# Weight sums of a seven-product matrix scheme: from VectorE additions to accumulating DMAs, with the signs of one operand row turned

## The chip, the cores and the metric

The kernel runs as one program on one core of a Trainium2 chip. The metric is the device time of one execution, in microseconds (us); lower is better. The kernel before takes 1967.14 us (median of three runs, 1966.62 to 1968.99). PE is the matrix engine, PEld its weight loads, DVE the vector engine, ACT the scalar engine, POOL the GpSimd engine and SP the engine that does nothing here but issue DMAs.

## The reference, cut to what matters

One step of a two-layer decoder trunk for 1024 prompt tokens and 8 times 8 sample tokens with the same weights, model width 1024, all in 32-bit floats. Each layer is a mixer followed by a dense SwiGLU FFN of inner width 2816. The change touches only the FFN:

```
def _swiglu_ffn(x, g, w_gate, w_up, w_down):
    h = _rmsnorm(x, g)
    return x + (jax.nn.silu(h @ w_gate) * (h @ w_up)) @ w_down
```

## The kernel before, in words

The activations lie transposed: model features on the 128 partitions, 1088 tokens (1024 + 64) along the free side. They are treated as two halves of 544 tokens, each of two chunks of 272. A first stage (up to about 390 us) does the input projection, convolution, attention and half of the output projection. After it come four passes (`half_pass`): layer 0 half 0, layer 0 half 1, layer 1 half 0, layer 1 half 1. Each pass goes through the 22 blocks of 128 FFN columns in 11 pairs j, so there are 44 pairs in all.

Every weight block is 128 x 1024 floats (512 KB). It is loaded from DRAM into a `raw` tile, and split into a high part `whi` (ACT, rounded to the float32r format) and a low part `wlo = raw - whi` (DVE). Every product is then three matmuls: high by high, high by low, low by high.

The gate and up products of one pair are computed as a Strassen-Winograd scheme. It has two halves of the contraction, two FFN blocks and two token chunks, and so 7 products where 8 would be plain. Its weight operands are A11, A12, S2, S1, S3, S4, A22. Of these A11, A12 and A22 are loaded blocks and four are sums made on DVE by whole-block operations, in `gate_up` of `Weights`: S1 = A21 + A22, S3 = A11 - A21, S2 = S1 - A11, S4 = A12 - S2. The activation operands B11, B21, T2, T1, T3, B22, T4 are made once for each pass by `operands`. One product is 2 x 4 x 3 = 24 matmuls of 272 columns.

A pair on PE is: seven products (items 0 to 6, which this text calls R11, R12, S2, S1, S3, S4, R22), then the down projection of the pair before (items D0 and D1, four groups of 12 matmuls each). That is 7 x 24 + 8 x 12 = 264 matmuls. `act` turns the results into hidden activations: for the last one, from product R22, ACT applies the silu out of PSUM (`t<-pp 128x272`), DVE multiplies (`t<-pp,t 128x272`), and the result is split into `hh` and `hl`. Each group of the down projection takes one of four PSUM tiles `pp` and is added to the residual by one DVE operation (`g<-pp,g` or `res<-pp,res`). The fourth group of a pair takes the tile that this last multiplication reads.

What sets the order: PE's order is as written. The other engines' orders come from the scheduler of the framework, which starts from program order. Each engine and each DMA queue runs in order, and waits by semaphores. There are six `whi`/`wlo` slots in rotation, so that the conversion of an item can begin once PE has finished the item six before it. `get` converts up to `LEAD` = 4 items ahead in program order. There are four `raw` tiles in rotation (pool `wraw`) and one separate tile for S1. All weight loads stand in SP's queue; a load waits until the tile that it fills has been converted. All of the trace's instructions go through a helper and so carry one line, L111; they are told apart by the names of their tiles.

Of the kernel before, what the change touches and what calls it, by code (L numbers as in the profile page):

```python
# [10 lines left out]
F32 = mybir.dt.float32  # L11
F32R = mybir.dt.float32r
BF16 = mybir.dt.bfloat16
AF = mybir.ActivationFunctionType
ALU = mybir.AluOpType
# [3 lines left out]
P = 128  # L19
# [26 lines left out]
PRE = (False, False, True, True)  # L46
NT = 7
LAG = 4000.0
LEAD = 4
NP = FT // 2  # L50
PROD = ('B11', 'B21', 'T2', 'T1', 'T3', 'B22', 'T4')
# [24 lines left out]
FFN = {}  # L76
# [4 lines left out]
POOLW = len(UNITS) + len(FFN)  # L81
OUTW = POOLW + 2


def r32(ap):
    return ap.bitcast(F32)


class Paced:
# [3 lines left out]
    def __init__(self, engine, rate, fixed):  # L93
        self.engine, self.rate, self.fixed, self.t = engine, rate, fixed, 0.0
# [20 lines left out]
class Weights:  # L115


    def __init__(self, nc, w_ap, raw_pool):
        self.nc, self.w, self.raw_pool = nc, w_ap, raw_pool
        self.slots = deque()  # L120
        self.loaded, self.next, self.ahead = deque(), 0, 1
        self.ready, self.todo, self.raws = deque(), deque(), {}

    def add_pool(self, pool, n, name):
        self.slots.extendleft((pool, f"{name}{i}") for i in range(n))
# [6 lines left out]
    def slot(self):  # L132
        pool, nm = self.slots[0]
        self.slots.rotate(-1)
        hi = pool.tile([P, 1024], F32R, tag=nm + "h", name="whi")
        lo = pool.tile([P, 1024], F32R, tag=nm + "l", name="wlo")
        return hi, lo
# [32 lines left out]
    def gate_up(self, l, j):  # L170


        r = {}

        def get(n):
            if n not in r:
                r[n] = self.raw(FFN[l, j, n])
            return r[n]

        def sums():  # L180
            for n in ('A21', 'A22'):
                get(n)
            r['S1'] = self.sums.tile([P, 1024], F32, tag="S1", name="S1")
            self.V.tensor_tensor(r['S1'], r['A21'], r['A22'], ALU.add)
            self.V.tensor_tensor(r['A21'], r['A11'], r['A21'], ALU.subtract)
            self.V.tensor_tensor(r['A11'], r['S1'], r['A11'], ALU.subtract)
            self.split(r['A11'])

        def s4():
            self.V.tensor_tensor(r['A12'], r['A12'], r['A11'], ALU.subtract)  # L190
            self.split(r['A12'])
        return [lambda: self.split(get('A11')), lambda: self.split(get('A12')), sums, lambda: self.split(r['S1']),
                lambda: self.split(r['A21']), s4, lambda: self.split(r['A22'])]

    def down(self, l, j):
        return [lambda: self.split(self.raw(FFN[l, j, 'D0'])), lambda: self.split(self.raw(FFN[l, j, 'D1']))]

    def pool(self, g):
        def f():
            t = self.raw_pool.tile([P, 1024], F32, tag="raw", name="raw")  # L200
            self.nc.sync.dma_start(out=t[:, :512], in_=self.w[POOLW + g // 2][:, g % 2 * 512:g % 2 * 512 + 512])
            self.split(t, 512)
        return [f]

    def out(self, o):
        return [lambda: self.split(self.raw(OUTW + o))]

    def advance(self):
        while self.todo and len(self.ready) < LEAD:
            self.todo.popleft()()  # L210

    def get(self):
        if not self.ready:
            self.todo.popleft()()
        u = self.ready.popleft()
        self.advance()
        return u
# [31 lines left out]
def _body(ctx, tc, I, O):  # L249
    nc = tc.nc  # L250
    V, S, T, G = Paced(nc.vector, 1.04, 175), Paced(nc.scalar, 0.85, 190), Paced(nc.tensor, 0, 0), nc.gpsimd
    cp = ctx.enter_context(tc.tile_pool(name="const", bufs=1))
    xp = ctx.enter_context(tc.tile_pool(name="xp", bufs=1))
    tp = ctx.enter_context(tc.tile_pool(name="tp", bufs=1))
    wraw = ctx.enter_context(tc.tile_pool(name="wraw", bufs=4))
    wa = ctx.enter_context(tc.tile_pool(name="wa", bufs=1))
    ps_pool = tc.tile_pool(name="ps", bufs=8, space=PSUM)
    ps = ps_pool.__enter__()
# [1 line left out]
    W = Weights(nc, I['w'], wraw)  # L260
# [5 lines left out]
    def pcol(name, i=0, n=1):  # L266
        return prm[:, PRM[name] + i:PRM[name] + i + n]
# [7 lines left out]
    def both():  # L275
        return pair_of(wide())

    def pair_of(t):
        return t[:, :2 * TW].rearrange("p (c t) -> p c t", c=2)
# [12 lines left out]
    def bank():  # L292
        return ps.tile([P, 512], F32, tag="ps", name="ps")

    def bank2():
        return pp.tile([P, 2, 512], F32, tag="pp", name="pp")[:, :, :TW]
# [426 lines left out]
    for t in range(4):  # L723
        b = bank()
# [111 lines left out]
    def rt(h, o):  # L836
        return res[h][o // 4][:, o % 4]
# [13 lines left out]
    def operands(h, goff):  # L851

        x, n = {}, {}

        def value(m, i):
            n[m] = slot(xp, i, 4, F32)
            return n[m]

        def norm(m, i, k, q):
            value(m, i)  # L860
            for j in range(4):
                kt = 4 * q + j
                V.scalar_tensor_tensor(n[m][:, j], pair_of(rt(h, kt))[:, k], pcol('norm_ffn', goff + kt), RS[h][:, k],
                                       ALU.mult, ALU.mult)

        def cut(m, i):
            x[m] = slot(xp, i, 4), slot(xp, i + 1, 4)
            split(x[m], n[m])

        def diff(m, a, b, i):  # L870
            out = n[i] if i in n else value(m, i)
            V.tensor_tensor(out, n[a], n[b], ALU.subtract)
            n[m] = out

        def job(f, *a):
            return lambda: f(*a)
        first = [job(norm, 'B11', 0, 0, 0), job(cut, 'B11', 2), job(norm, 'B21', 14, 0, 1), job(cut, 'B21', 4)]
        rest = [job(norm, 'B12', 1, 1, 0), job(diff, 'T1', 'B12', 'B11', 12), job(norm, 'B22', 10, 1, 1),
                job(diff, 'T2', 'B22', 'T1', 13), job(cut, 'T2', 6), job(cut, 'T1', 8), job(diff, 'T4', 'B21', 'T2', 0),
                job(diff, 'T3', 'B22', 'B12', 'B12'), job(cut, 'B22', 12), job(cut, 'T3', 10), job(cut, 'T4', 14)]  # L880
        return x, deque(first), deque(rest)

    hold.append(True)
    ua = W.take(4)
    for o in range(KT):
        b = bank2()
# [13 lines left out]
    for k in range(2):  # L900
        for o in range(KT):
            b = bank2()
            mm3(b[:, k], [(wcol(u, o), Y(4 + j, k)) for j, u in enumerate(uc)])
            r = pair_of(rt(0, o))[:, k]
# [9 lines left out]
            if k and o == 1:  # L914
                X, build, rest = operands(0, 0)
# [6 lines left out]


    hp = ctx.enter_context(tc.tile_pool(name="h", bufs=1, side="right"))
    W.sums = hp
    hist = [hp.tile([P, 16 + PB + TW], F32, name=f"hist{i}") for i in range(2)]
    for t in hist:
        V.memset(t[:, 0:16], 0.0)
# [4 lines left out]
    def product(out, w, x, s, start, stop):  # L933

        for kt in range(4):
            wh, wl = (t[:, s * 512 + kt * P:s * 512 + kt * P + P] for t in w)
            xh, xl = (t[:, kt, :] for t in x)
            T.matmul(out=out, lhsT=wh, rhs=xh, start=start and kt == 0, stop=False, skip_group_check=True)
            T.matmul(out=out, lhsT=wh, rhs=xl, start=False, stop=False, skip_group_check=True)
            T.matmul(out=out, lhsT=wl, rhs=xh, start=False, stop=stop and kt == 3, skip_group_check=True)  # L940

    def gate_up(x):

        h = [[hp.tile([P, 2, TW], F32R, tag="h" + n, bufs=4, name="h" + n) for n in 'hl'] for _ in range(2)]

        def keep(src):
            t = both()
            S.activation(t, src, AF.Copy)
            return t

        def act(f, k, src, kept):

            if kept is None:
                g = both()
                S.activation(g[:, 0], src[:, 0], AF.Silu)
                V.tensor_tensor(g[:, 0], src[:, 1], g[:, 0], ALU.mult)
            else:
                g = kept
                V.tensor_tensor(g, src, g, ALU.add)
                S.activation(g[:, 0], g[:, 0], AF.Silu)  # L960
                V.tensor_tensor(g[:, 0], g[:, 0], g[:, 1], ALU.mult)
            split((h[k][0][:, f, :], h[k][1][:, f, :]), g[:, 0])

        def step(i, dst=None):
            w = W.get()
            start = dst is None
            if start:
                dst = bank2()
            for s in range(2):
                product(dst[:, s], w, x[PROD[i]], s, start, True)  # L970
            flush()
            return dst
        a = step(0)
        p1 = keep(a)
        b = step(1)
        act(0, 0, b, p1)
        step(2, a)
        u2 = keep(a)
        c = step(3)
        p5 = keep(c)  # L980
# [133 lines left out]
    def half_pass(l, half, x, pooled, after, following, mixed=False):  # L1114
# [4 lines left out]
        for j in range(NP):  # L1119
# [28 lines left out]
            if j:  # L1148
                down(half, last, beside=steps)
# [157 lines left out]
```

## Time and profile before

| | |
|---|---|
| median of three runs | 1967.14 us |
| profiled execution, its own time | 1965.52 us |
| its span in the trace | 1963.7 us |
| PE busy | 1887.9 us, 96% |
| PEld busy | 1835.1 us, 93% |
| DVE busy | 1670.9 us, 85% |
| ACT busy | 940.5 us, 48% |
| POOL busy | 32.6 us, 2% |
| granted TensorE clock, mean | 0.99 |
| DMA | 177.75 MB, mean 91 GB/s |

The median and the profiled execution differ by 1.6 us. The busy shares are means over the span; the rows further below show single stretches. In the rows of waits, "PE pp <- DVE res" means that PE was idle until a DVE instruction that touches `res` released it.

### The profile page before, as it was taken

To read this page: it belongs to the slowest core of one execution; us is meant where nothing else is said; L and a number is where in the kernel's file an instruction comes from. 1 tells how busy PE (TensorE), PEld (TensorE's weight loads), DVE (VectorE), ACT (ScalarE), POOL (GpSimd) and SP (SyncE) were. 2 spreads that over 40 slices of the span, in tenths; PEclk is the share of its full clock that TensorE was granted. 3 is DMA by queue.
4 is the path that set the end of the run, shared out by engine and by line. 5 is a ranking of instruction groups with operands and counts; after the bars stand their busy time and mean duration, and the time that the engine had idled before them with its cause. 6 is when DMAs were issued, how large, how long until landed. Compare 5 with 4: busy or idle time off the path is not lost.

```text
span 1963.7 us, 34755 instructions
## 1 busy us (share of the span) xinstructions
PE 1887.9 (96%) x14437; PEld 1835.1 (93%) x14437; DVE 1670.9 (85%) x2593; ACT 940.5 (48%) x1609; POOL 32.6 (2%) x47
## 2 busy tenths in 40 slices
PE   7999889799999999899999998999999999999999
PEld 6998568799999999799999998999999999999999
DVE  6999999999778785998988889989898897778784
ACT  7345784544343453564454454544444544443432
POOL 1100000000000000000000000000000000000000
PEclk9999998899999999999999999999999999999999
DMA  5310103132232341132232321323323223232321
GB/s 194 94 59 1 47 15 110 41 99 97 88 106 86 108 156 65 44 103 97 93 112 76 113 97 44 117 90 108 106 77 114 98 93 125 89 106 86 108 86 68
DMA packets 52479, 177.75 MB, mean 91 GB/s; under 512 B 6000, under 2 KB 10704, under 8 KB 51776
## 3 DMA queue, kind: packets, MB, share of 16 engines
q1 hardware_dynamic: 50960, 172.12, 26.2%
q0 software_dynamic: 1360, 3.40, 0.9%
q8 instruction: 113, 1.85, 0.4%
q14 instruction: 46, 0.38, 0.1%
HBM read 169.74 MB, written 6.74 MB: 90 GB/s over the span
## 4 chain that ended last, share of the span: by engine, by line
PE 84%; DVE 10%; ACT 3%; DMA 2%; issue 1%; SPq 0%; ACTq 0%; DVEq 0%
PE pp L111 74%; PE ps L111 10%; DVE x L111 3%; DVE wlo L111 2%; DVE res L111 1%; DVE ca L111 1%; ACT P L111 1%; DMA raw<-w 1%; ACT t L111 1%; DVE g L111 1%; DVE raw L111 1%; DVE t L111 1%; DVE ss L111 1%; ACT x L111 0%; DMA x<-x 0%
## 5 line engine op out<-in xcount | busy, mean ns | idle before, releaser
L111 PE MATMUL pp<-x,whi 128*128 128x272 f32 x5568 | 1069.1, 291 | 25.3 <-ACT t L111 5.9
L111 PEld LDWEIGHTS pp<-x,whi 128*128 128x128 f32 x5568 | 884.5, 190 | 31.1 <-ACT t L111 7.4
L111 PE MATMUL pp<-x,wlo 128*128 128x272 f32 x2784 | 810.7, 291 | 0.6 <-DVE wlo L111 0.4
L111 ACT ACTIVATE whi<-raw 128x1024 fp32r<-128x1024 f32 (+1 forms) x390 | 407.5, 1048 | 520.4 <-PE pp L111 353.3
L111 DVE TENSOR_TENSOR wlo<-raw,whi 128x1024 fp32r<-128x1024 f32 (+1 forms) x386 | 466.5, 1212 | 113.5 <-ACT whi L111 112.6
L111 PEld LDWEIGHTS pp<-x,wlo 128*128 128x128 f32 x2784 | 528.6, 190 | 1.6 <-DVE wlo L111 1.6
L111 PE MATMUL pp<-hh,whi 128*128 128x272 f32 x1408 | 408.4, 290 | 6.6 <-DVE res L111 4.3
L111 PE MATMUL pp<-hh,wlo 128*128 128x272 f32 x1408 | 407.6, 289 | 0.0
L111 PE MATMUL pp<-hl,whi 128*128 128x272 f32 x1408 | 405.7, 288 | 0.0
L111 PEld LDWEIGHTS pp<-hh,whi 128*128 128x128 f32 x1408 | 265.3, 188 | 8.6 <-DVE res L111 4.4
L111 PEld LDWEIGHTS pp<-hl,whi 128*128 128x128 f32 x1408 | 265.4, 188 | 0.0
L111 PEld LDWEIGHTS pp<-hh,wlo 128*128 128x128 f32 x1408 | 264.9, 188 | 0.0
L111 PE MATMUL ps<-x,whi 128*128 128x272 f32 x896 | 178.5, 297 | 7.0 <-ACT whi L111 7.0
L111 DVE TENSOR_TENSOR g<-pp,g 128x544 f32<-128x544 f32 x184 | 129.9, 722 | 43.0 <-PE pp L111 42.5
L111 PEld LDWEIGHTS ps<-x,whi 128*128 128x128 f32 x896 | 143.9, 190 | 13.1 <-ACT whi L111 7.0
L111 DVE TENSOR_TENSOR res<-pp,res 128x544 f32<-128x544 f32 (+1 forms) x200 | 136.3, 698 | 13.9 <-PE pp L111 13.0
L111 DVE TENSOR_TENSOR t<-pp,t 128x544 f32<-128x544 f32 (+1 forms) x176 | 114.4, 651 | 38.5 <-PE pp L111 38.1
L111 PE MATMUL ps<-x,wlo 128*128 128x272 f32 x448 | 130.4, 291 | 0.4 <-DVE wlo L111 0.4
L111 ACT ACTIVATE hh<-t 128x272 fp32r<-128x272 f32 x176 | 74.6, 426 | 108.8 <-DVE t L111 107.9
L111 ACT ACTIVATE t<-t 128x272 f32<-128x272 f32 x170 | 71.8, 427 | 98.3 <-DVE t L111 97.7
L111 DVE TENSOR_TENSOR raw<-raw 128x1024 f32<-128x1024 f32 x88 | 107.5, 1221 | 0.0
L111 ACT ACTIVATE t<-pp 128x544 f32<-128x544 f32 (+1 forms) x176 | 96.9, 551 | 12.9 <-PE pp L111 12.8
(166 smaller groups left out, 1534.0 us busy)
## 6 DMA issues: line engine op xcount, KB each, us to landing
raw<-w SPq DMA_DIRECT2D x294, 512.0 KB, 3.3
x<-x SPq DMA_DIRECT2D x16, 272.0 KB, 8.5
res<-x SPq DMA_DIRECT2D x2, 1088.0 KB, 6.3
g<-x SPq DMA_DIRECT2D x2, 1088.0 KB, 6.0
o_y<-res SPq DMA_DIRECT2D x4, 544.0 KB, 2.7
raw<-w SPq DMA_DIRECT2D x8, 256.0 KB, 3.0
o_y<-g SPq DMA_DIRECT2D x2, 544.0 KB, 3.2
o_y<-g SPq DMA_DIRECT2D x4, 272.0 KB, 2.1
```

What stands on the lines that cost most here:

```text
L111: return f(*a, **k)
```

## The change

The four sums are no longer computed on DVE. For each sum the first block is loaded into a `raw` tile through SP's queue as before, and then a second block is added to it by a DMA that accumulates (`accum_op=add`), issued by POOL. Its source is DRAM (A22 onto A21 for S1, A21 onto A11 for S3) or another `raw` tile (S1 onto A11 for S2, S2 onto A12 for S4). So A11, A12, A21 and A22 are loaded seven times in all for one pair where they were loaded four times. Only additions occur, so signs are turned in the activations: B11 is stored negated (`cut` with sign -1), T1, T2 and T3 are formed with the other sign, and one addition in `act` becomes a subtraction.

The fetch of an item (its load and its accumulating DMA) is now separate from its conversion, and `convert` issues fetches up to `AHEAD` = 2 items in front of the conversion. The pool of `raw` tiles has five instead of four; the separate S1 tile is gone.

```diff
-        def sums():
-            for n in ('A21', 'A22'):
-                get(n)
-            r['S1'] = self.sums.tile([P, 1024], F32, tag="S1", name="S1")
-            self.V.tensor_tensor(r['S1'], r['A21'], r['A22'], ALU.add)
-            self.V.tensor_tensor(r['A21'], r['A11'], r['A21'], ALU.subtract)
-            self.V.tensor_tensor(r['A11'], r['S1'], r['A11'], ALU.subtract)
-            self.split(r['A11'])
-
-        def s4():
-            self.V.tensor_tensor(r['A12'], r['A12'], r['A11'], ALU.subtract)
-            self.split(r['A12'])
-        return [lambda: self.split(get('A11')), lambda: self.split(get('A12')), sums, lambda: self.split(r['S1']),
-                lambda: self.split(r['A21']), s4, lambda: self.split(r['A22'])]
+        def made(n, first, *added):
+            def fetch():
+                r[n] = self.raw(FFN[l, j, first])
+                for a in added:
+                    self.nc.gpsimd.dma_start(out=r[n], in_=r[a] if a in r else block(a), accum_op=ALU.add)
+            return fetch, lambda: self.split(r[n])
+        a11, a12, a22 = made('R11', 'A11'), made('R12', 'A12'), made('R22', 'A22')
+        s1, s3 = made('S1', 'A21', 'A22'), made('S3', 'A11', 'A21')
+        s2, s4 = made('S2', 'A11', 'S1'), made('S4', 'A12', 'S2')
+
+        def s1s2():
+            s1[0]()
+            s2[0]()
+        return [a11, a12, (s1s2, s2[1]), (lambda: None, s1[1]), s3, s4, a22]
...
+    def convert(self):
+
+        while self.todo and self.fetched <= AHEAD:
+            if self.fetched == len(self.todo):
+                break
+            self.todo[self.fetched][0]()
+            self.fetched += 1
+        self.todo.popleft()[1]()
+        self.fetched -= 1
...
-    wraw = ctx.enter_context(tc.tile_pool(name="wraw", bufs=4))
+    wraw = ctx.enter_context(tc.tile_pool(name="wraw", bufs=5))
...
+        def cut(m, i, sign=1.0):
             x[m] = slot(xp, i, 4), slot(xp, i + 1, 4)
-            split(x[m], n[m])
...
+            if sign > 0:
+                split(x[m], n[m])
+            else:
+                S.activation(x[m][0], n[m], AF.Copy, scale=-1.0)
+                V.scalar_tensor_tensor(x[m][1], n[m], -1.0, r32(x[m][0]), ALU.mult, ALU.subtract)
...
-                V.tensor_tensor(g, src, g, ALU.add)
+                V.tensor_tensor(g, src, g, ALU.subtract)
```

POOL's queue in the changed kernel, two pairs of the last pass (before, nothing of this stood there): the additions that make S1, S2, S3 and S4, in this order.

```order
L183 DMA raw_19629<-w 128x1024
L183 DMA raw_19632<-raw_19629 128x1024
L183 DMA raw_19701<-w 128x1024
L183 DMA raw_19764<-raw_19632 128x1024
L183 DMA raw_20000<-w 128x1024
L183 DMA raw_20003<-raw_20000 128x1024
L183 DMA raw_20072<-w 128x1024
L183 DMA raw_20135<-raw_20003 128x1024
```

In the second pair raw_20000 is S1, raw_20003 S2, raw_20072 S3 and raw_20135 S4; each second row reads the tile that the row before the pair of rows has filled, so S2's addition follows S1's and S4's follows S2's.

ACT in the kernel before, from the last pass, at the end of the seven products of a pair: S1_20236 is S1, raw_20162 is S2, t_20227 the last silu, read from PSUM.

```order
L111 ACTIVATE hh_19996<-t_20125 128x272
L111 ACTIVATE t_20092<-t_20092 128x272
L111 ACTIVATE whi_20300<-S1_20236 128x1024
L111 ACTIVATE hh_19996<-t_20092 128x272
L111 ACTIVATE t_20227<-pp_20002 128x272
L111 ACTIVATE whi_20240<-raw_20162 128x1024
L111 ACTIVATE hh_19994<-t_20227 128x272
L111 ACTIVATE whi_20364<-raw_20232 128x1024
```

The same place in the changed kernel: raw_20003 is S2, raw_20000 is S1, t_20067 the last silu.

```order
L112 ACTIVATE hh_19829<-t_19963 128x272
L112 ACTIVATE whi_20075<-raw_20003 128x1024
L112 ACTIVATE t_19930<-t_19930 128x272
L112 ACTIVATE hh_19829<-t_19930 128x272
L112 ACTIVATE whi_20138<-raw_20000 128x1024
L112 ACTIVATE t_20067<-pp_19837 128x272
L112 ACTIVATE hh_19827<-t_20067 128x272
L112 ACTIVATE whi_20204<-raw_20072 128x1024
```

Before, one conversion (S1) stood in front of the last silu and S2's behind it; now S2's conversion and then S1's both stand in front of it. DVE's order moves in the same way: the low parts of S2 and S1 now precede the multiplication that follows this silu and the residual additions behind it, and the four whole-block sums are gone from between them.

## Rows read from the trace of the kernel before

**Rows 1.** The page, part 1: busy us, share, instructions.

```profile
PE 1887.9 (96%) x14437; PEld 1835.1 (93%) x14437; DVE 1670.9 (85%) x2593; ACT 940.5 (48%) x1609; POOL 32.6 (2%) x47
```

**Rows 2.** Busy time by stretch; after the engines: granted clock, DMA share, GB/s.

```profile
390.00:1963.70 1573.70, 1544.08 (x12155) 1537.53 (x12153) 1310.66 (x1786) 716.84 (x1078) 14.84 (x17) 1.00 0.29 96
...
1700.00:1900.00 200.00, 200.00 (x1589) 200.00 (x1588) 153.94 (x193) 83.79 (x121) 0.00 (x0) 1.00 0.29 95
```

**Rows 3.** What PE waited for, 390 us to the end: total us, times, longest.

```profile
PE pp L111 <- DVE res L111: 7.4, 8, 1.9
PE pp L111 <- DVE t L111: 6.3, 4, 2.7
PE pp L111 <- ACT t L111: 5.9, 5, 3.1
PE pp L111 <- DVE g L111: 4.1, 3, 1.8
PE pp L111 <- DVE ss L111: 1.6, 1, 1.6
```

**Rows 4.** Instruction groups by form, DVE: count, busy us, mean ns, idle before.

```profile
L111 DVE TENSOR_TENSOR raw<-raw 128x1024 f32<-128x1024 f32 x88 | 107.5, 1221 | 0.0
...
L111 DVE TENSOR_TENSOR S<-raw 128x1024 f32<-128x1024 f32 x44 | 53.9, 1224 | 30.0 <-DMA raw<-w 29.9
L111 DVE TENSOR_TENSOR raw<-S,raw 128x1024 f32<-128x1024 f32 x44 | 53.7, 1221 | 0.0
```

**Rows 5.** Chain that ended last: first and last weight sum in it.

```profile
1185.99 1.13 DVE S L111
...
1583.58 1.13 DVE raw L111
```

**Rows 6.** Timeline of ACT in the last pass: start us, length us.

```profile
1780.97 1.06 ACT L111 ACTIVATE whi<-raw 128x1024 fp32r<-128x1024 f32 x1 [4.99 <-PE pp L111]
1783.98 1.06 ACT L111 ACTIVATE whi<-raw 128x1024 fp32r<-128x1024 f32 x1 [1.95 <-PE pp L111]
...
1801.19 0.43 ACT L111 ACTIVATE t<-t 128x272 f32<-128x272 f32 x1 [1.69 <-DVE t L111]
1802.15 1.06 ACT L111 ACTIVATE whi<-S 128x1024 fp32r<-128x1024 f32 x1 [0.53 <-PE pp L111]
1803.12 0.41 ACT L111 ACTIVATE hh<-t 128x272 fp32r<-128x272 f32 x1
1803.44 0.38 ACT L111 ACTIVATE t<-pp 128x272 f32<-128x272 f32 x1
```

**Rows 7.** Timeline of DVE in the same stretch.

```profile
1785.07 1.23 DVE L111 TENSOR_TENSOR wlo<-raw,whi 128x1024 fp32r<-128x1024 f32 x1 [1.78 <-ACT whi L111]
...
1788.10 1.23 DVE L111 TENSOR_TENSOR wlo<-raw,whi 128x1024 fp32r<-128x1024 f32 x1 [0.22 <-ACT whi L111]
...
1802.21 0.43 DVE L111 TENSOR_TENSOR t<-t 128x272 f32<-128x272 f32 x1
...
1804.05 0.44 DVE L111 TENSOR_TENSOR t<-pp,t 128x272 f32<-128x272 f32 x1
```

**Rows 8.** Timeline of all engines: the down projection's first weight load.

```profile
1801.89 0.19 PEld L111 LDWEIGHTS pp<-hh,whi 128*128 128x128 f32 x1
```

**Rows 9.** DMA: a queue's packets, MB, share; issues with KB each, us to landing.

```profile
q1 hardware_dynamic: 50960, 172.12, 26.2%
...
raw<-w SPq DMA_DIRECT2D x294, 512.0 KB, 3.3
...
o_v_old<-cv_nat POOLq DMA_DIRECT2D x1, 480.0 KB, 7.7
...
o_conv_p<-g POOLq DMA_DIRECT2D x4, 15.0 KB, 1.9
```

**Rows 10.** Timeline of POOL: what one DMA takes it.

```profile
54.63 0.59 POOL L555 DMA_DIRECT2D o_conv_p<-g  x1 [5.54 <-DVE exts L111]
...
55.30 0.92 POOL L556 DMA_DIRECT2D o_conv_s<-exts  x1
```

More of the change, by code (lines that the diff above doesn't have):

```diff
@@ L48 @@
 LAG = 4000.0
+AHEAD = 2
 LEAD = 4
@@ L121, in __init__ @@
         self.loaded, self.next, self.ahead = deque(), 0, 1
-        self.ready, self.todo, self.raws = deque(), deque(), {}
+        self.ready, self.todo, self.fetched = deque(), deque(), 0
     def add_pool(self, pool, n, name):
@@ L173, in gate_up @@
         r = {}
[L175 to L178, printed above, removed]
-        def sums():
-            for n in ('A21', 'A22'):
-                get(n)
-            r['S1'] = self.sums.tile([P, 1024], F32, tag="S1", name="S1")
-            self.V.tensor_tensor(r['S1'], r['A21'], r['A22'], ALU.add)
-            self.V.tensor_tensor(r['A21'], r['A11'], r['A21'], ALU.subtract)
-            self.V.tensor_tensor(r['A11'], r['S1'], r['A11'], ALU.subtract)
-            self.split(r['A11'])
@@ L189, in s4, with block @@
-        def s4():
-            self.V.tensor_tensor(r['A12'], r['A12'], r['A11'], ALU.subtract)
-            self.split(r['A12'])
-        return [lambda: self.split(get('A11')), lambda: self.split(get('A12')), sums, lambda: self.split(r['S1']),
-                lambda: self.split(r['A21']), s4, lambda: self.split(r['A22'])]
+        def block(n):
+            return self.w[FFN[l, j, n]]
+        def made(n, first, *added):
[4 more added lines that the diff above has]
+            return fetch, lambda: self.split(r[n])
@@ new lines, in gate_up, with block, fetch @@
+        a11, a12, a22 = made('R11', 'A11'), made('R12', 'A12'), made('R22', 'A22')
[5 more added lines that the diff above has]
+        return [a11, a12, (s1s2, s2[1]), (lambda: None, s1[1]), s3, s4, a22]
+    def block(self, i, n=1024):
+        r = []
+        def fetch():
+            t = self.raw_pool.tile([P, 1024], F32, tag="raw", name="raw")
+            self.nc.sync.dma_start(out=t[:, :n], in_=self.w[i] if isinstance(i, int) else i)
+            r.append(t)
+        return [(fetch, lambda: self.split(r[0], n))]
@@ L195, in down @@
     def down(self, l, j):
-        return [lambda: self.split(self.raw(FFN[l, j, 'D0'])), lambda: self.split(self.raw(FFN[l, j, 'D1']))]
+        return self.block(FFN[l, j, 'D0']) + self.block(FFN[l, j, 'D1'])
     def pool(self, g):
[L199 to L203, printed above, removed]
-    def out(self, o):
-        return [lambda: self.split(self.raw(OUTW + o))]
+        return self.block(self.w[POOLW + g // 2][:, g % 2 * 512:g % 2 * 512 + 512], 512)
@@ L208, in advance @@
+    def out(self, o):
+        return self.block(OUTW + o)
+    def convert(self):
[6 more added lines that the diff above has]
+        self.fetched -= 1
     def advance(self):
         while self.todo and len(self.ready) < LEAD:
-            self.todo.popleft()()
+            self.convert()
     def get(self):
@@ L213, in get @@
         if not self.ready:
-            self.todo.popleft()()
+            self.convert()
         u = self.ready.popleft()
@@ L864, in norm, with mix @@
                                        ALU.mult, ALU.mult)
-        def cut(m, i):
+        def cut(m, i, sign=1.0):
             x[m] = slot(xp, i, 4), slot(xp, i + 1, 4)
-            split(x[m], n[m])
-        def diff(m, a, b, i):
+            if sign > 0:
[3 more added lines that the diff above has]
+                V.scalar_tensor_tensor(x[m][1], n[m], -1.0, r32(x[m][0]), ALU.mult, ALU.subtract)
+        def mix(m, a, b, i, op=ALU.subtract):
             out = n[i] if i in n else value(m, i)
-            V.tensor_tensor(out, n[a], n[b], ALU.subtract)
+            V.tensor_tensor(out, n[a], n[b], op)
             n[m] = out
@@ L876, in job @@
             return lambda: f(*a)
[L877 to L880, printed above, removed]
+        first = [job(norm, 'B11', 0, 0, 0), job(cut, 'B11', 2, -1.0), job(norm, 'B21', 14, 0, 1), job(cut, 'B21', 4)]
+        rest = [job(norm, 'B12', 1, 1, 0), job(mix, 'T1', 'B11', 'B12', 12), job(norm, 'B22', 10, 1, 1),
+                job(mix, 'T2', 'B22', 'T1', 13, ALU.add), job(cut, 'T2', 6), job(cut, 'T1', 8),
+                job(mix, 'T4', 'B21', 'T2', 0), job(mix, 'T3', 'B12', 'B22', 'B12'), job(cut, 'B22', 12),
+                job(cut, 'T3', 10), job(cut, 'T4', 14)]
         return x, deque(first), deque(rest)
@@ L924, in _body @@
     hp = ctx.enter_context(tc.tile_pool(name="h", bufs=1, side="right"))
-    W.sums = hp
     hist = [hp.tile([P, 16 + PB + TW], F32, name=f"hist{i}") for i in range(2)]
```

## The prediction, made before the changed kernel ran

> **What bounds the kernel now.** I read the busy shares first [rows 1]: PE is busy 96% of the span and DVE 85%. The means hide two kinds of stretch, so the windows come next [rows 2]. In the last pass (1700 to 1900 us) PE is busy for all 200 us while DVE has 46 us free. PE alone sets the pace there, at 200 / 1589 = 0.126 us for a matmul, so a pair of 264 matmuls takes 33.2 us, a product (24) 3.02 us and a group of the down projection (12) 1.51 us. Over the four passes together PE idles 1573.7 - 1544.1 = 29.6 us. The waits of PE [rows 3] name DVE for 19.4 us of that and ACT for 5.9 us, 25.3 us together. None of these waits lies after 1700 us: they stand where the passes meet, where DVE also has the norms and the pooling to do. So work taken from DVE can win at most some 25 us of 1965, though the work itself is large.
>
> **What is removed.** The sums are 88 + 44 + 44 = 176 whole-block DVE instructions of 1.22 us [rows 4], 215 us in all. Nearly all of it lies beside PE. What stood on the path to the end is read from the chain: 12 of its pieces are weight sums, the first and the last in [rows 5], at 1.13 to 1.22 us, 13.7 us together. The bounds of this gain are 0 (the next item of DVE's queue is late in its place) and 25.3 us (every wait of rows 3 goes). I take 13.7 us, since the removed pieces were counted on the path itself.
>
> **What is added on DVE, ACT and POOL.** The turned signs replace instructions one for one, and the negated split occurs once a pass: taken as nothing, hidden by DVE's freed time. POOL issues 176 accumulating DMAs. A DMA of 128 rows takes it 0.59 us [rows 10], so about 104 us on an engine that is 98% idle: nothing by itself, but each DMA waits in POOL's queue for the load before it.
>
> **What is added on the DMA engines.** A load of 512 KB lands 3.3 us after its issue [rows 9]. Its share of the engines: 0.262 x 16 x 1963.7 us for 172.12 MB is 47.8 engine-us per MB, so 25 for 0.524 MB, or 1.57 us of all sixteen. A pair had 6 loads (9.4 us of 33.2). It now has 9 loads (14.1 us) and four accumulating DMAs, each of which must read two blocks; at twice 1.57 that is 12.6 us more, 26.7 us in all, 80% of the pair. It fits, but no longer leaves the loads alone.
>
> **The new wait: S2.** S2 = A11 + (A21 + A22) is made by a load, an addition, and a second addition that waits for the first. I follow it in the last pass, in us from the start of R11 on PE. The down projection begins at 1801.9 to 1802.0 [rows 8], seven products earlier is 1780.9, and the ACT row at 1780.97, released by PE, agrees [rows 6]. With five tiles and nine tile uses in a pair, S1's load takes the tile of R22, whose low part ends at 1785.07 + 1.23 = 1786.3 [rows 7]: 5.4. S2's load takes the tile converted next (1788.10 + 1.23: 8.4) and is not late. So S1's block lands at 5.4 + 3.3 = 8.7, and with L for one accumulating DMA from issue to landing S2 is ready at 8.7 + 2L.
>
> When is it due? PE itself needs S2 only some 20 us later, but ACT and DVE run in order, and S2's conversion now stands in front of the last silu. From its start X: conversion 1.06 (ACT), low part 1.22 (DVE; X + 2.3), multiplication of the silu before 0.43 (X + 2.7), its `hh` 0.41 (X + 3.1), conversion of S1 1.06 (X + 4.2), the last silu 0.38 (X + 4.6); meanwhile DVE has S1's low part to X + 5.4, then the last multiplication 0.44, X + 5.9, and 0.1 for the hops between engines: X + 6.0 [rows 6, 7]. That frees the PSUM tile which the fourth group of the down projection needs at 21.1 + 3 x 1.51 = 25.6. Behind the same DVE queue wait the residual additions of the groups. So X may be 19.6 at the latest, and the chain fits for 2L up to 10.9, L up to 5.4 us.
>
> L is not in the trace. Its bounds: 3.3 us, a plain load of as many bytes, and 7.7 us, the slowest POOL-issued DMA of nearly that size, a DRAM to DRAM copy of 480 KB [rows 9]. Between them I build it from rows: 1.9 us for a 15 KB DMA of 128 rows from POOL, which is all fixed cost, plus two reads at 1.57 = 5.0, plus half of one load's 1.57 for the loads that cross it (S2's and S3's during the first addition, S4's and R22's during the second), 5.8 rounded up. Then S2 is ready at 8.7 + 11.5 = 20.2, 0.6 us late, in each pair: 44 x 0.6 = 26 us. With the lower bound it is ready at 15.3 and costs nothing; with the upper at 24.1, 4.5 us late, 198 us.
>
> S3 and S4 have more room: S3 is due only when the second down block starts (27.2), S4 at the next pair. The loads of D0 and D1 take the tiles of S2 and S1 and wait for S4's addition too, but PE needs them a pair later. POOL's queue also holds the pooling state's DMAs of the third pass; in four pairs they stand between S4's addition and the next S1's, a gap of about 19 us, and wait for DVE. Taken as nothing; up to 5 us each, 20 in all, if the gap doesn't cover them.
>
> **Sum**, on the profiled execution: 1965.5 - 13.7 + 26 = 1978. Its own time stands 1.6 us under the median of the runs, so 1980 us.
>
> A rule that speaks against the change: by the Trainium skill (SBUF — State Buffer, SBUF: two separate sides) a POOL-issued DMA cannot have its descriptors written while DVE runs an instruction in a two-port mode; a DMA of 620 ns took 3100 ns there. The rows of POOL don't show it: 0.59 and 0.92 us [rows 10], with DVE busy most of the time. The same page gives `tensor_tensor`, which is what DVE mostly runs here, no such mode, so I hold it for unlikely and price it below from rows.
>
> **The rivals.**
> A. The chain fits: L is 5.4 us or less, because the crossing loads don't slow it or the two reads overlap. For it: the loads take only 29% of the DMA engines now [rows 2], and 0.6 us of lateness is smaller than my error on L. Then only the gain is left: 1965.5 - 13.7 + 1.6 = 1953 us.
> B. The accumulating DMA is slow in itself, at the upper bound L = 7.7 us or beyond. For it: nothing in the trace shows a DMA that adds. Then 1965.5 - 13.7 + 198 + 1.6 = 2151 us. PE stands 4.5 us before the fourth group of every pair. It decides from L = 5.4 on, by 88 us for each further us of L.
> C. DVE holds up POOL's descriptors: each addition waits out one block instruction of DVE, 1.22 us [rows 4], so S2 comes 2.4 us later than in the forecast, 44 x 3.0 = 132 us: 2086 us. Against it stand rows 10.
>
> **How the numbers follow.** The forecast (S2 late by 0.1 to 1.6 us in a pair, 1958 to 2025 us) has 0.40, A 0.40, B 0.15, C 0.05. No change means within 0.2% of 1967.1, 1963.2 to 1971.1, which is about what a measurement can tell. A is faster with 0.36 of its 0.40 and the rest no change (a gain near 0). The forecast is faster in 0.04, no change in 0.08, slower in 0.28. B and C are slower. That is 0.40 faster, 0.12 no change, 0.48 slower. The range goes from 1948 us (A with some 5 us more gain) to 2115 us, which takes in C and a part of B. The forecast's own range is 1958 to 2025 us.
>
> **What would show each step.** DVE's busy time should fall by about 215 us to some 1455 us, and POOL's rise to about 135 us. The weight loads number 294 + 3 x 44 = 426, and DMA's share in the last pass rises from 0.29 towards 0.8. L is read directly as issue to landing of POOL's `raw<-w` and `raw<-raw`: 5.8 us expected, 5.4 or less for A, 7.7 or more for B. In the last pass PE is no longer busy for all 200 us in the forecast, B and C: a wait of about 0.6, 4.5 or 3.0 us in each pair, before the down projection's groups, released by DVE, with ACT's conversion of S2 waiting for a DMA. For A the last pass stays at 200 us. POOL DMA instructions longer than 0.6 us would show C. The prediction is wrong in its frame if PE waits elsewhere, above all at the products for `wlo`, or if loads on SP's queue, not the additions, come late.

## The result, and the profile after

The changed kernel takes 2217.19 us (median of four runs, 2208.32 to 2225.48); the kernel before, run beside it, 1966.88 us. The ratio is 1.128, with a 95% interval of 1.125 to 1.130. It is slower, as forecast, but by 250 us and not by 13, and the time lies above the range. The profiled execution took 2225.5 us.

The page after. First the busy shares, then the two DMA queues (packets, MB, share of sixteen engines), then the DMA issues (count, KB each, us from issue to landing):

```profile
PE 1967.5 (88%) x14437; PEld 1905.5 (86%) x14437; DVE 1496.5 (67%) x2417; ACT 938.3 (42%) x1609; POOL 185.6 (8%) x223
...
q1 hardware_dynamic: 69968, 241.33, 32.6%
q0 software_dynamic: 26704, 95.69, 24.0%
...
raw<-w SPq DMA_DIRECT2D x426, 512.0 KB, 3.9
raw<-w POOLq DMA_DIRECT2D x88, 512.0 KB, 8.0
raw<-raw POOLq DMA_DIRECT2D x88, 512.0 KB, 5.7
```

Against [rows 1, 9], DVE does less and POOL more, as the change says. What is odd is PE: it issues the same 14437 matmuls and is busy 80 us longer. The queue q0 holds the additions (92.3 of its 95.69 MB). It takes 0.240 x 16 x 2223.7 / 95.69 = 89 engine-us for a MB, q1 takes 48: an added byte costs 1.86 times a loaded one, which is near the factor of two that was assumed.

The windows after, from 390 us to the end and for 200 us of the last pass (busy us and matmuls of PE first; at the end granted clock, DMA share, GB/s):

```profile
390.00:2223.00 1833.00, 1621.98 (x12171) 1607.41 (x12171) 1144.51 (x1617) 718.11 (x1082) 162.64 (x187) 0.94 0.63 168
1950.00:2150.00 200.00, 184.20 (x1376) 183.11 (x1375) 112.26 (x145) 73.13 (x107) 18.14 (x21) 0.94 0.68 178
```

Against [rows 2] this splits the loss. PE is idle 1833 - 1622 = 211 us where it was idle 29.6: 181 us more. And it is busy 1622 us for the work of 1544: 78 us more, at a granted clock of 0.94 instead of 1.00. Together these are the 260 us by which the span grew, all but a microsecond. PE's waits over the whole span (us, times, longest) have at their head two names of [rows 3], grown:

```profile
PE pp L112 <- DVE t L112: 165.5, 37, 13.5
PE pp L112 <- ACT t L112: 29.8, 6, 9.1
```

One pair of the last pass shows how. PE's timeline (start and length in us) has its first product R11 from 2020.50 on:

```profile
2020.50 0.42 PE L112 MATMUL pp<-x,whi 128*128 128x272 f32 x2
```

S1's block is loaded through SP's queue. The view of this load alone gives its time from issue to landing:

```profile
2025.99 0.33 SPq L130 DMA_DIRECT2D raw<-w  x1
...
DMA to landing us min/median/max: 3.2/3.2/3.2
```

POOL's timeline (in brackets the idle time before and what ended it) has S1's addition and then S2's, and the views of these two alone give their times to landing:

```profile
2029.93 0.86 POOL L183 DMA_DIRECT2D raw<-w  x1 [24.15 <-DVE t L112]
2036.58 0.86 POOL L183 DMA_DIRECT2D raw<-raw  x1 [5.79 <-DMA raw<-w]
...
DMA to landing us min/median/max: 6.0/6.0/6.0
...
DMA to landing us min/median/max: 7.4/7.4/7.4
```

ACT's timeline has S2's conversion, which waited for the addition, and the last silu:

```profile
2044.08 1.06 ACT L112 ACTIVATE whi<-raw 128x1024 fp32r<-128x1024 f32 x1 [5.20 <-DMA raw<-raw]
...
2048.07 0.38 ACT L112 ACTIVATE t<-pp 128x272 f32<-128x272 f32 x1
```

And PE's timeline has the fourth group of the down projection:

```profile
2046.08 0.29 PE L112 MATMUL pp<-hh,wlo 128*128 128x272 f32 x1
2049.82 0.39 PE L112 MATMUL pp<-hh,whi 128*128 128x272 f32 x1 [3.45 <-DVE t L112]
...
2050.67 0.43 PE L112 MATMUL pp<-hh,wlo 128*128 128x272 f32 x1
2050.89 0.43 PE L112 MATMUL pp<-hh,whi 128*128 128x272 f32 x1
```

S1's block lands at 2029.2, 8.7 us after R11's start, as was worked out. POOL issues S1's addition 0.7 us later. The addition lands after 6.0 us, at 2035.9, and POOL issues S2's addition another 0.7 us later. That one lands after 7.4 us. So S2's conversion starts at X = 23.6 where 20.2 was forecast and 19.6 allowed, 4.0 us late, and PE waits 3.45 us, in front of the group that the prediction named. After the wait the matmuls come every 0.22 to 0.23 us instead of 0.126: 272 columns in 0.227 us is the 1.2 GHz level, after a stretch at 2.4. The granted clock, the third number from the end, agrees:

```profile
2020.80:2046.00 25.20, 25.20 (x202) 25.20 (x202) 12.48 (x15) 10.67 (x15) 3.44 (x4) 1.00 0.73 188
2050.00:2054.50 4.50, 4.50 (x25) 4.50 (x26) 3.83 (x6) 1.29 (x2) 0.00 (x0) 0.62 0.66 235
```

The next pair's R11 starts at 2059.0, so this pair took 38.5 us for 33.2; of the difference 3.45 are waiting and some 1.6 slow clock.

### The profile page after: what moved, and what is told of

Same layout as the page of the kernel before. It is cut to its first block, busy times and chain, and to the rows that moved or that the text cites. A ratio compares the mean times of both kernels' runs of the same rounds, so it can differ in the third digit from the quotient of the medians.

```text
span 2223.7 us, 35573 instructions
## 1 busy us (share of the span) xinstructions
PE 1967.5 (88%) x14437; PEld 1905.5 (86%) x14437; DVE 1496.5 (67%) x2417; ACT 938.3 (42%) x1609; POOL 185.6 (8%) x223
## 3 DMA queue, kind: packets, MB, share of 16 engines
q0 software_dynamic: 26704, 95.69, 24.0%
## 5 line engine op out<-in xcount | busy, mean ns | idle before, releaser
L112 ACT ACTIVATE whi<-raw 128x1024 fp32r<-128x1024 f32 (+1 forms) x434 | 453.8, 1048 | 824.4 <-PE pp L112 381.3
L112 DVE TENSOR_TENSOR wlo<-raw,whi 128x1024 fp32r<-128x1024 f32 x430 | 520.4, 1213 | 411.3 <-ACT whi L112 411.1
L112 PE MATMUL pp<-hh,whi 128*128 128x272 f32 x1408 | 440.4, 313 | 166.4 <-DVE t L112 161.2
L112 PEld LDWEIGHTS pp<-hh,whi 128*128 128x128 f32 x1408 | 293.1, 208 | 176.6 <-DVE t L112 168.7
L112 PE MATMUL pp<-hl,whi 128*128 128x272 f32 x1408 | 431.8, 307 | 0.0
L112 PEld LDWEIGHTS pp<-hl,whi 128*128 128x128 f32 x1408 | 293.1, 208 | 0.0
L112 PEld LDWEIGHTS pp<-hh,wlo 128*128 128x128 f32 x1408 | 291.3, 207 | 0.0
L183 POOL DMA_DIRECT2D raw<-w x88 | 79.9, 908 | 1038.9 <-DVE t L112 472.6
L183 POOL DMA_DIRECT2D raw<-raw x88 | 75.7, 860 | 517.8 <-DMA raw<-w 160.2
L112 DVE TENSOR_TENSOR hl<-t,hh 128x272 fp32r<-128x272 f32 x176 | 77.0, 438 | 57.6 <-ACT hh L112 57.4
```

The costliest lines, as they stand in the source:

```text
L112: return f(*a, **k)
L183: self.nc.gpsimd.dma_start(out=r[n], in_=r[a] if a in r else block(a), accum_op=ALU.add)
```

## The experiments

Each time stands beside runs of the kernel before on the same chip, so the ratio (95% interval) is what counts. Where nothing else is said, the edit is made in the changed kernel.

**e1, no chain.** S2's second addition no longer waits for the first (the sums get other values):

```diff
-        s2, s4 = made('S2', 'A11', 'S1'), made('S4', 'A12', 'S2')
+        s2, s4 = made('S2', 'A11', 'A22'), made('S4', 'A12', 'S2')
```

> The changed kernel, but S2's addition reads A22 from DRAM instead of the S1 tile, so the two additions no longer stand in series (S2 and what follows from it hold other values; as many additions, loads and bytes). Theory 'series': S2 is late because two additions run one after the other. Then S2 is ready about 8.7 + 7.5 = 16 us into a pair, before the 19.6 us at which it delays ACT; the wait of 2 to 4 us before the fourth down group is gone in the plain pairs, the clock goes back to 0.98 or more, only the pairs with pooling state in POOL's queue still wait: 1955 to 2000 us. Rival 'traffic': the additions slow the DMA engines and all loads come late. The bytes are the same, so 2150 to 2225 us.

2108.29 us, ratio 1.073 (1.070 to 1.075): between both. Without the series 109 of the 250 us go, but S2 is still late: its addition now runs beside S1's and takes longer. ACT in the last pass, and PE behind it:

```profile
1835.99 1.06 ACT L112 ACTIVATE whi<-raw 128x1024 fp32r<-128x1024 f32 x1 [2.29 <-DMA raw<-w]
```

```profile
1841.73 0.39 PE L112 MATMUL pp<-hh,whi 128*128 128x272 f32 x1 [0.55 <-DVE t L112]
```

S2's addition was issued at 1827.72 and took 8.2 us. X is 20.65 here (R11 at 1815.34), and PE waits 0.55. Both pairs give the same due time: 23.6 - 3.45 and 20.65 - 0.55 are 20.1, where 19.6 was worked out.

**e2, loads only.** All loads and turned signs stay, the additions are left out (so the sums lack their second blocks):

```diff
-                for a in added:
+                for a in ():
```

> The changed kernel without any accumulating DMA: the seven loads of a pair are converted as they are (the sums are left out, other values). It shows what the freed DVE is worth and what the three further loads cost. Both theories: no wait in the plain pairs. If the gain of 13.7 us of the prediction is real, 1953 us (1945 to 1960); if DVE's queue is late for other reasons, 1967; if the further loads cost anything by themselves, more than 1970.

1951.15 us, ratio 0.9925 (0.9906 to 0.9945). The relief of DVE is real, the 132 more loads cost nothing that shows beside it, and the whole loss lies in the additions. PE in the third and last pass (as in the windows above):

```profile
1300.00:1700.00 400.00, 400.00 (x3173) 399.84 (x3172) 304.80 (x448) 185.84 (x287) 7.70 (x9) 1.00 0.46 149
1700.00:1900.00 200.00, 200.00 (x1589) 200.00 (x1588) 129.81 (x170) 83.30 (x121) 0.00 (x0) 1.00 0.43 143
```

**e3, early.** The same transfers, with S1 and S2 fetched ahead of R11:

```diff
-        return [a11, a12, (s1s2, s2[1]), (lambda: None, s1[1]), s3, s4, a22]
+        def first():
+            s1s2()
+            a11[0]()
+        return [(first, a11[1]), a12, (lambda: None, s2[1]), (lambda: None, s1[1]), s3, s4, a22]
```

> The changed kernel with the loads and additions of S1 and S2 put in front of R11's load instead of behind R12's, nothing else. S1's load then takes a tile that is free two items (about 6 us or more) earlier. 'Series': S2 is ready at about 15 us into a pair instead of 23, within its 19.6; no wait in plain pairs, clock 0.98 or more, 1955 to 1985 us, the rest from POOL's queue in the third pass. 'Traffic': the same bytes and the same number of DMAs, 2150 to 2225 us.

2011.82 us, ratio 1.024 (1.022 to 1.027). 205 of 250 us go, by moving the start of these fetches and nothing else:

```profile
1300.00:1700.00 400.00, 370.56 (x2869) 369.54 (x2870) 282.56 (x419) 171.98 (x264) 45.30 (x52) 0.96 0.74 191
1700.00:1900.00 200.00, 200.00 (x1590) 200.00 (x1589) 130.03 (x169) 83.07 (x121) 19.87 (x23) 1.00 0.77 204
```

In the last pass PE is busy for all 200 us at full clock, beside DMA engines at 0.77. So neither traffic nor the transfers as such slow PE or its clock in a plain pair; late S2 did. What is left stands in the third pass.

**e4, traffic beside.** The kernel before, with 110 additions of 480 KB from DRAM into a tile that nothing reads (`extra`), one behind the other from 341 to 1055 us on POOL's queue.

> The kernel before, with 110 accumulating DMAs of 128 x 960 floats from DRAM into a tile that nothing reads, one after the other through POOL's queue from the start of the first pass on (some 600 us of them, more additions per pair than the changed kernel has). 'Series': they stand in nobody's way, PE stays busy and the time is that of before, 1962 to 1972 us. 'Traffic': the loads of the first pass come late, PE waits 3 us or more in each of some 18 pairs, 2020 us or more.

1984.44 us, ratio 1.0095 (1.0072 to 1.0118), between both again. Traffic costs some 19 us over about 700 us, though here about 5 additions fall into a pair, not four. Loads beside it land in 4.1 us instead of 3.3, and an addition that crosses only loads takes 5.4:

```profile
raw<-w SPq DMA_DIRECT2D x294, 512.0 KB, 4.1
...
extra<-w POOLq DMA_DIRECT2D x110, 480.0 KB, 5.4
```

The window from 390 to 700 us lies wholly beside these additions. DVE is busy for 252.9 of its 310 us (82%):

```profile
390.00:700.00 310.00, 304.47 (x2374) 302.28 (x2373) 252.89 (x326) 136.52 (x196) 41.74 (x49) 0.99 0.75 171
```

**e5, another queue for the pooling state.** The third pass was still unexplained. Its DMAs of the pooling state move from POOL's queue to ACT's:

```diff
-                G.dma_start(out=O['pool_s'][:, kt], in_=es[:, :, DEC:])
+                nc.scalar.dma_start(out=O['pool_s'][:, kt], in_=es[:, :, DEC:])
```

(and in the same way the loads into `es` and the store of `halo`).

> The changed kernel with the DMAs of the pooling state (es, o_pool_s, o_pool_p) issued by ACT instead of POOL, nothing else. If POOL's queue is what makes three pairs of the third pass wait 11 to 13.5 us where the plain pairs wait 3.5, these come down to 3.5: about 28 us of idle time and some 7 us of low clock less, 2180 us (2160 to 2195). If the long waits have another cause (DVE's pooling work), 2205 to 2225.

2208.05 us, ratio 1.123 (1.119 to 1.126). The place in the queue is worth some 9 us, not 37: this explanation of mine fell. POOL's rows in a pair of the third pass show that S1's addition took 15 us (14.8 to its landing) though nothing stood ahead of it:

```profile
1402.17 0.87 POOL L183 DMA_DIRECT2D raw<-w  x1 [27.28 <-DVE wlo L112]
1417.59 0.86 POOL L183 DMA_DIRECT2D raw<-raw  x1 [14.54 <-DMA raw<-w]
```

It was not alone. Two plain loads that SP issued at 1401.58 and 1402.84 took 9.9 and 14.4 us in the same trace, and the two stores of the pooling state that ACT had issued at 1397.84 and 1398.27 took 11.9 and 12.2.

**e6, S2's second sum on DVE.** Of S2's addition nothing is left but a DVE instruction in front of its conversion:

```diff
-        s2, s4 = made('S2', 'A11', 'S1'), made('S4', 'A12', 'S2')
+        s2, s4 = made('S2', 'A11'), made('S4', 'A12', 'S2')
+        def s2c():
+            self.V.tensor_tensor(r['S2'], r['S2'], r['S1'], ALU.add)
+            s2[1]()
```

> The changed kernel, but S2's addition (and only that) is made by DVE again, in front of its conversion; S1, S3 and S4 by accumulating DMAs. 'Late S2': S2 is ready about 8.7 + 6.5 + 1.2 = 16.4 us into a pair, within 19.6; the plain pairs don't wait, only the pairs with pooling state in POOL's queue and the first pairs of a pass do: 1970 to 2020 us, clock 0.98. 'Traffic': three of four additions are left, so three quarters of the loss, 2130 to 2170 us.

2088.03 us, ratio 1.062 (1.059 to 1.064): better than the change, worse than expected. DVE runs in order too, and now itself waits for S1's addition (213.0 us between 390 and 1900 us).

**e7 and e8, edits together.** e7 is e3 with e5; e8 is e7 with e6.

> Both edits together: S1 and S2 fetched in front of R11, and the pooling state's DMAs on ACT's queue. With S2 early and POOL's queue free, what is left over the kernel with loads alone (1951 us) is the traffic, 15 to 20 us by the kernel with additions that nobody reads: 1971 us (1960 to 1985). If another wait takes over in the third pass, 1990 to 2012 us.

> The three edits together: S1 and S2 fetched in front of R11, pooling state's DMAs on ACT's queue, S2's addition on DVE. Three additions in a pair instead of four, 54 us of DVE work back, beside PE. Expected 1958 us (1950 to 1968), faster than the kernel before by about 0.4%; if the traffic of three additions still costs as much as that of four, 1970 us.

e7: 2004.79 us, ratio 1.020 (1.018 to 1.023); e8: 2055.58 us, 1.045 (1.043 to 1.047). Both missed. e8 has fewer additions than e7 and is slower; DVE's waits, 390 to 1900 us, point to the reason: the sum on DVE stands in front of other work and waits, mostly for S1's addition and now and then for S2's load. Behind it PE's waits for ACT's silus grow, from 21.5 us in e7 to 58.4:

```profile
DVE raw L112 <- DMA raw<-w: 128.4, 34, 8.8
...
PE pp L112 <- ACT t L112: 58.4, 31, 4.9
```

**e9, short additions.** The same 176 additions at the same places, each of a quarter of the columns:

```diff
-                    self.nc.gpsimd.dma_start(out=r[n], in_=r[a] if a in r else block(a), accum_op=ALU.add)
+                    self.nc.gpsimd.dma_start(out=r[n][:, :256], in_=(r[a] if a in r else block(a))[:, :256], accum_op=ALU.add)
```

> As the changed kernel, with the same 176 additions at the same places of POOL's queue, but each over 256 of the 1024 columns only (three quarters of every sum are left out). If the length of the addition decides (theory), L falls to some 3 us, S2 is ready at about 8.7 + 6 = 15 us after R11's start, before its 19.6, the waits of the plain pairs vanish and the last pass has PE busy for 200 of 200 us at clock 1.00; with what is left of the waits in the third pass 1950 to 1990 us. If the order of POOL's queue, the number of DMAs or the tiles held longer decides (rival), the waits stay and it takes 2100 us or more.

2019.99 us, ratio 1.029 (1.026 to 1.032): above the theory's 1990. The plain pairs are as the theory has it, the third pass is dearer. PE's windows in the third and the last pass:

```profile
1300.00:1700.00 400.00, 366.62 (x2839) 365.16 (x2839) 278.71 (x417) 169.90 (x263) 47.02 (x54) 0.96 0.52 149
1700.00:1900.00 200.00, 200.00 (x1590) 200.00 (x1589) 130.16 (x169) 83.01 (x120) 20.72 (x24) 1.00 0.54 159
```

POOL's timeline, a pair with pooling and then a plain one:

```profile
1385.04 0.90 POOL L1093 DMA_DIRECT2D o_pool_s<-es  x1 [6.99 <-DVE t L112]
1385.93 0.96 POOL L183 DMA_DIRECT2D raw<-w  x1
1393.04 0.86 POOL L183 DMA_DIRECT2D raw<-raw  x1 [6.15 <-issue]
...
1779.25 0.86 POOL L183 DMA_DIRECT2D raw<-w  x1 [21.84 <-DVE t L112]
1783.58 0.86 POOL L183 DMA_DIRECT2D raw<-raw  x1 [3.46 <-DMA raw<-w]
```

In the plain pair S1's short addition lands after 3.7 us and POOL issues S2's 0.7 us later. S2's conversion starts at 1788.93, X = 19.0 (R11 at 1769.9), before the 20.1 of the change and e1, and PE does not wait. In the pair with pooling S1's load took 7.1 us, beside a store of the pooling state. The first addition then stands behind a second store and takes 6.6 us, and PE waits 8.8 us.

**e10 to e12, the parts that could stay.** e10 has the turned signs alone, with the sums on DVE as before. e11 makes S4 alone by an accumulating transfer, issued as soon as DVE has S2 (`self.nc.gpsimd.dma_start(out=r['A12'], in_=r['A11'], accum_op=ALU.add)` in the place of DVE's addition). e12 makes S3 so, too.

> The turned signs alone: the weight sums are made by VectorE as before, with additions, four tiles, no accumulating transfer. Theory: the signs cost nothing, 1967 us (1963 to 1971). Rival: the negated split or the other form of the sums costs in each pass, 1975 us or more.

> The turned signs, and of the weight sums only S4 made by an accumulating transfer (A12's tile += S2's tile, issued as soon as VectorE has made S2); S1, S2, S3 stay on VectorE, four tiles, no further load. Theory (a late addition in front of in-order engines is what costs): S4 has about three products (9 us) of room more than one addition takes, so no wait comes, and a quarter of the 13.7 us is won: 1964 us (1960 to 1968). Rival (accumulating traffic costs wherever it is): 44 additions of 2.9 us of all DMA engines cost some 0.8 us each, 1975 us or more.

> As the run with S4 alone, and S3 too by an accumulating transfer (A21's tile += A11 from DRAM, issued as soon as VectorE has made S1). Theory: S3 is converted two products after S2, so its addition has some 6 us of room; half of the 13.7 us is won: 1960 us (1954 to 1967). If S3's addition comes late now and then, 1967 to 1985 us. Rival (traffic costs wherever it is): 1985 us or more.

e10: 1967.13 us, ratio 1.0002 (0.9987 to 1.0016): the signs are free. e11: 1976.85 us, 1.0056 (1.0040 to 1.0072); e12: 1979.21 us, 1.0067 (1.0051 to 1.0082). Both are slower than before, and no sum moved to a transfer beat the kernel before. e11 lies on the rival's side, but e12, with twice the additions, costs only 2 us more and stays under the rival's 1985, so neither side holds as it was put. No wait in e11 is longer than 3.3 us; from 390 to 1900 us it has 98 matmuls fewer than e10, worth 12 us. That is 4.5 us of short waits more (PE busy 1480.94 us against 1485.40), and the rest slower matmuls.

**e13 and e14, the pooling state again.** On e9: e13 leaves out the eight stores `o_pool_s` (an output is not written); e14 makes the edit of e5.

> As the run with additions over 256 of 1024 columns (2020 us), and the eight stores of the pooling state (o_pool_s) are left out too. If these stores (their place in POOL's queue or their many packets) hold S1's addition in the third pass, the three long waits there (8 to 12 us each) vanish and the time falls by 31.8 us of waits plus the slow clock behind them, some 40 us: 1980 us (1970 to 1990). If the waits there come from something else (VectorE's pooling work, the extra tiles), 2010 us or more.

> As the run with additions over 256 of 1024 columns (2020 us), with all transfers of the pooling state issued from ScalarE's queue; their packets stay. If the place in POOL's queue is what costs, as without the stores: 1980 us (1970 to 1990). If it is the DMA engines that the small packets occupy, the waits stay: 2005 to 2020 us. In between, both.

e13: 1976.75 us, ratio 1.0052 (1.0032 to 1.0072), within its theory's bounds. e14: 2006.82 us, 1.022 (1.018 to 1.027), so the larger part is not the queue. In e14 two stores leave ACT at 1443.42 and 1445.21, and POOL's rows behind them read:

```profile
1450.51 0.86 POOL L183 DMA_DIRECT2D raw<-w  x1 [29.43 <-DVE t L112]
1460.20 0.86 POOL L183 DMA_DIRECT2D raw<-raw  x1 [8.83 <-DMA raw<-w]
```

S1's short addition lands after 9.1 us with nothing ahead of it in its queue, against 3.7 in e9's last pass. The DMA queues between 1435 and 1475 us (packets, MB, share of the engines):

```profile
q1 hardware_dynamic: 1440, 4.98, 49.1%
q10 hardware_dynamic: 4160, 0.25, 9.1%
```

The queue of the pooling state, q10, has 4160 packets of 60 bytes (two loads and two stores): 0.25 MB take 0.091 x 16 x 40 = 58 engine-us, almost five times what 48 engine-us for a MB would make of them. While the two stores are under way the engines are busy for 0.95 of the time and move 148 GB/s, and four plain loads take 9.6 us (median), where all loads of this run take 3.7:

```profile
1445.00:1458.00 13.00, 12.91 (x103) 12.70 (x102) 7.15 (x10) 5.53 (x10) 0.86 (x1) 1.00 0.95 148
...
raw<-w SPq DMA_DIRECT2D x4, 512.0 KB, 9.6
```

So loads and additions alike land late beside these packets, whatever queue issued them.

**e15 and e16, sums on GpSimd's own arithmetic.** The signs of e10; e15 makes S4 by `nc.gpsimd.tensor_tensor`, e16 all four sums. No transfer is added.

> The turned signs with S4 alone made by GpSimd's own tensor_tensor, issued where the run with S4 alone by transfer issued it; no accumulating transfer, no further load. Theory (the 10 us that 44 accumulating transfers cost are DMA traffic): no traffic, a quarter of VectorE's relief, 1963 us (1959 to 1968). Rival (they are the price of S4 made off VectorE, with its tile held longer): 1975 us or more.

> The turned signs with all four sums made by GpSimd's tensor_tensor in the old order. If GpSimd makes one in about 2.5 us, S2 is ready some 7.5 us after its blocks and in most pairs late for the in-order conversions: 2000 us or more (theory of lateness). Rival (GpSimd is quick enough or the conversions wait anyway): VectorE's relief is won whole, 1951 to 1960 us.

e15: 2015.83 us, ratio 1.025 (1.023 to 1.026), far on the rival's side; e16: 2263.76 us, 1.151 (1.149 to 1.154), on the side of the theory of lateness. In e15 something else came in, and it is in e16 too (`hl<-t,hh`, 446 ns in e15, takes 891 there), so that e16 does not show lateness by itself. DVE's groups by form in e15 (count, busy us, mean ns):

```profile
L111 DVE TENSOR_TENSOR wlo<-raw,whi 128x1024 fp32r<-128x1024 f32 x378 | 473.7, 1256 | 118.2 <-ACT whi L111 117.8
...
L111 DVE TENSOR_TENSOR wlo<-S,whi 128x1024 fp32r<-128x1024 f32 x44 | 101.4, 2305 | 12.1 <-ACT whi L111 12.0
```

The split of S1, which starts beside GpSimd's addition (2490 ns), takes 2305 ns instead of some 1223 (the same split's mean over raw tiles in the kernel before); DVE's operations out of PSUM, `g<-pp,g` at 712 ns, are not slowed. By the Trainium skill (SBUF — State Buffer, SBUF: two separate sides) DVE and GpSimd share a port pair, and a DVE operation with two SBUF inputs and a GpSimd operation that reads SBUF shut each other out; the 2305 ns agree. So e15 does not tell what the 10 us of e11 are.

## Why the prediction was wrong

In per cent of 1967 us, the ratios make a stair: e2 -0.75, e13 +0.52, e9 +2.88, the change +12.76. The steps are -15 us (relief of DVE), +25 (176 short additions), +46 (the pooling state's stores beside them), +194 (additions of full length), each to some 3 to 8 us; together 250. e2 has these stores and e13 has not, so the 25 us are a little too small by whatever the stores cost without additions.

- **The gain** of 13.7 us, the signs and the three extra loads at nothing: right (e2, e10).
- **The place** was right: S2's conversion, in order on ACT ahead of the last silu, holds the PSUM tile of the fourth down group. The due time of 19.6 was off by 0.5 us, and S1's block landed at 8.7 as worked out.
- **The step that failed is 8.7 + 2L = 20.2**, the time at which S2 is ready. It was 23.6 in the pair shown, 3.4 us later, and in 44 pairs that is 150 us. Of the 3.4 us 1.9 are L, the time of one addition. S1's took 6.0 us, near the 5.8 of the sum (which went on with 11.5 for two, where twice 5.8 is 11.6), but S2's took 7.4. The sum let half of one load cross an addition; S2's addition took 5.5 us (median of 12 pairs) where two loads crossed it and 7.2 (24 pairs) where three did, as in the pair shown, each time with S3's addition beside it too. What of this is the loads and what S3's addition was not separated. The other 1.4 us were put at nothing: from the landing of S1's load to POOL's issue of S1's addition, and from that addition's landing to the issue of S2's, 0.7 us pass each time, and the formula has S2's addition start when S1's lands. What POOL does in them the rows don't show; in e4, where the additions only follow one another, it is 0.35 us.
- **The mechanism** was the forecast's and rival B's alike, an S2 that is late in each pair, and only the size decided. The waits of the first name read 165.5 us, between the forecast's 26 and B's 198. The range cut B off at 2115. B's 2151 comes nearest to the time, in part by luck: its L of 7.7 was longer than either addition of the pair, which made up for some of what it left out (the next two points).
- **A term was missing**: what a wait costs behind its end. Behind each wait of 3 us or more at least eleven matmuls came at the 1.2 GHz level, and PE's busy time, mostly by this, grew by 78 us beside the 181 of idle time. Rival B too was priced without it. e3, with the same transfers, and e9, with short ones, show it to follow from the waits: in their last pass PE does not wait and the clock stays 1.00.
- **The pooling state's DMAs**, "taken as nothing; up to 5 us each, 20 in all", cost some 46 us even beside short additions. Only 13 of them are the place in POOL's queue, which was the mechanism thought of (e14); the rest goes with the stores whatever queue issues them, and by the rows of e14 it is that thousands of 60-byte packets hold the DMA engines.
- **Rival C** had named a sign, POOL DMA instructions longer than 0.6 us, and it came: the additions' rows stand at 0.85 to 1.2 us. But a plain DMA of [rows 10] took 0.92, so the sign tells nothing. What speaks against C is e4: there DVE is busy for 82% of the time, and an addition takes 5.4 us, with none of DVE's block operations of 1.22 us added. **Rival A** needed L of 5.4, and would have missed the third pass.
- **Readings named ahead**: 426 loads as said. DMA share 0.68: with the measured 1.86 for the factor of two the sum of 26.7 us becomes 25.8, over 38.5 us of the longer pair 0.67. POOL's 185.6 us instead of 135 come from 0.87 us per accumulating DMA. DVE fell by 174 us instead of 215: lengths of neighbouring DVE instructions overlap in the trace, and the busy time counts an overlap once (added up singly, they fall by 223 us, from 1852 to 1629).

Left open: the 25 us of the short additions and the 10 us of e11. They are short waits and slower matmuls. PE's waits from 390 us on come to 33.4 us in e13 and to 16.7 in e2. Those of more than half a microsecond that e11 has and e10 has not, or shorter, are four (1.5 to 3.3 us); all stand between 1215 and 1495 us, in the third pass. The cost hardly grows with the number of additions (44 in e11, 88 in e12), and what makes it was not found.

## What to carry to other kernels

A transfer that computes is worth what its start allows: here the same bytes cost 205 us less when their fetch was issued some products earlier. Before an operation moves from an engine to a DMA, work out when its result is due through every in-order engine behind it, take the transfer's time beside the traffic that it brings, count what passes between a landing and the issue that waits for it, and add to each wait of PE the slow clock that follows. Where the margin is under the uncertainty of one unknown duration, its upper end belongs in the range.

## What the runs showed of the hardware

An accumulating DMA of 480 KB from DRAM takes 5.4 us where it crosses only loads (e4); in the changed kernel those of 512 KB take 8.0 us (median, from DRAM) and 5.7 (from another tile), 6.0 and 7.4 in the pair shown. An added byte costs the DMA engines 1.86 times a loaded one. The issue takes POOL 0.86 us, where plain DMAs took 0.59 and 0.92 [rows 10], and it comes 0.7 us after the landing that it waits for (0.35 in e4). One store of 60 KB in 60-byte packets takes 9.8 us (e14, median of eight) beside the loads. GpSimd needs 2.49 us for a 128x1024 addition (e15), and a DVE split with two SBUF inputs that starts beside it takes 2.31 us instead of 1.22.
